# The first group of a seven-product matmul: half of its contraction by plain products in the order of arrival, and B loaded one block of rows at a time

## The chip, the cores and the metric

The kernel runs on one core of a Trainium2 chip. The time is the device time of the launch in microseconds (us), as a median of several executions. Ratios between kernels are the mean time of one kernel's fast runs over the mean of the other's in the same rounds, with a 95% interval, so they are not quite the ratio of the medians quoted beside them. Engines are named as in the profile: PE is TensorE, PEld its weight loads, DVE is VectorE, ACT is ScalarE, POOL is GpSimd. POOL issues the loads here.

## The reference

```python
m, k, n = 4096, 4096, 4096          # a and b: standard normal, float32
x = np.matmul(a, b)
return 0.5 * x * (1 + np.tanh(np.sqrt(2 / np.pi) * (x + 0.044715 * x**3)))
```

## The kernel before

Both matrices are cut into two by two quadrants, and each quadrant product is built from seven half-size products of sums instead of eight plain ones. The output is done in 16 groups of four 512 x 512 tiles (one in each quadrant). A group has 7 products; each runs over a contraction of 2048 in four quarters of 512, and a quarter is 16 matmuls of 128 x 128 by 128 x 512. DVE makes the fp16 sums of the operands (`aS`, `bS`) two steps ahead, and after each product DVE and ACT fold the result into the outputs (`settle`).

```python
PRODUCTS = [
    ("Y", "11", ("12", "22", 1)),          # needs B12 and B22 for its first sum
    ("X", ("11", "12", -1), "22"),
    ("X", ("12", "22", -1), ("21", "22", 1)),
    ("X", ("11", "22", -1), ("11", "22", -1)),
    ("X", "22", ("21", "11", 1)),
    ("Y", ("22", "21", -1), "11"),
    ("Y", ("21", "11", -1), ("11", "12", 1)),
]
```

A tile of A or B is 1024 contraction rows by 512, 1.05 MB in fp16, cast from float32 by the DMA. A tile of A is turned by a DVE transposition after it has landed. A tile of B comes in eight pieces of 128 KB: 32 partitions with 4 rows each.

```python
b_v = b.rearrange("(c g jj q e) n -> c g e q jj n", g=4, q=Q, e=2, jj=NJ // 2)   # Q = 32
...
for g in range(4):
    for e in range(2):
        nc.gpsimd.dma_start(
            out=t[g * Q : (g + 1) * Q, e::2, :],
            in_=b_v[kh * CH + c, g, e, :, :, n0 : n0 + NC],
        )
```

So partition 32 g + q holds the rows 256 g + 64 jj + 2 q + e of its chunk. That odd order is what the transposition of A gives, and B has to follow it.

Of the kernel before, what the change touches and what calls it, by code (L numbers as in the profile page):

```python
# [7 lines left out]
F32 = mybir.dt.float32  # L8
F16 = mybir.dt.float16
BF16 = mybir.dt.bfloat16  # L10
# [3 lines left out]
ALU = mybir.AluOpType  # L14
AX = mybir.AxisListType

P = 128
Q = 32
NC = 512
KC = 1024  # L20
NJ = KC // P
RUN = KC // 4
RT = 4
TM = RT * P
AHEAD = 2
# [12 lines left out]
]  # L38
NP = len(PRODUCTS)
QPH = 4  # L40


SQUARE_MAX = 2.0**26
# [45 lines left out]
def half_path(  # L89
# [9 lines left out]
    nc = tc.nc  # L99
    M, K = a.shape  # L100
    _, N = b.shape
# [3 lines left out]
    CH = KH // KC  # L105

    pool = ctx.enter_context(tc.tile_pool(name="sb", bufs=1))
    psum_pool = ctx.enter_context(tc.tile_pool(name="psum", bufs=1, space=bass.MemoryType.PSUM))
# [7 lines left out]
    checks = {which: iter(range(stats[which].shape[1] // NX)) for which in stats}  # L116

    a_v = a.rearrange("(x mm) (c g r) -> c g mm x r", mm=Q, g=4, r=RUN)
    b_v = b.rearrange("(c g jj q e) n -> c g e q jj n", g=4, q=Q, e=2, jj=NJ // 2)

    a_tiles, b_tiles = {}, {}
    a_slot = {"11": 0, "12": 1, "22": 2, "21": 3}
    b_slot = {"12": 0, "22": 1, "21": 2, "11": 3}
# [22 lines left out]
    def load_b(nb, quad, c):  # L146
        kh, jh = int(quad[0]) - 1, int(quad[1]) - 1
        n0 = jh * NH + nb * NC
        t = pool.tile([P, NJ, NC], F16, name="bR", tag=f"bR{b_slot[quad]}{c}")
        for g in range(4):  # L150
            for e in range(2):
                nc.gpsimd.dma_start(  # L152
                    out=t[g * Q : (g + 1) * Q, e::2, :],
                    in_=b_v[kh * CH + c, g, e, :, :, n0 : n0 + NC],
                )
        b_tiles[nb, quad, c] = t

    def part(tiles, blk, quad, q):

        t = tiles[blk, quad, q // 2].rearrange("p x y -> p (x y)")  # L160
        w = 4 * NC
        return t[:, (q % 2) * w : (q % 2 + 1) * w]

    energy, squares = {}, []
    W = 2 * NC
# [82 lines left out]
    def make_sums(mb, nb, s, q):  # L248
        _, oa, ob = PRODUCTS[s]
        got = []  # L250
        for tiles, blk, o, tag in ((a_tiles, mb, oa, "aS"), (b_tiles, nb, ob, "bS")):
            if isinstance(o, str):
                got.append(part(tiles, blk, o, q))
                continue
            t = pool.tile([P, 4 * NC], F16, name=tag, tag=tag, bufs=AHEAD + 1)
            nc.vector.tensor_tensor(  # L256
                out=t[:, :], in0=part(tiles, blk, o[0], q), in1=part(tiles, blk, o[1], q),
                op=ALU.add if o[2] > 0 else ALU.subtract,
            )
            got.append(t)  # L260
        sums[mb, nb, s, q] = got

    groups = []
# [5 lines left out]
    banks = {}  # L269
    post = {}  # L270

    def multiply(gi, s, q):
        mb, nb = groups[gi]
        chain = PRODUCTS[s][0]
        first = q == 0 and (s == 0 or s == 1)
        sa, sb = sums.pop((mb, nb, s, q))
        sa = sa.rearrange("p (jj m e) -> p jj m e", jj=2, e=2)
        sb = sb.rearrange("p (kt n) -> p kt n", n=NC)
        for i in range(RT):
            if first:  # L280
                par = (gi + (chain == "Y")) % 2
                banks[chain, i] = psum_pool.tile([P, NC], F32, name=f"acc{chain}", tag=f"bank{par}{i}")
            for j in range(4):
                nc.tensor.matmul(  # L284
                    banks[chain, i][:, :],
                    sa[:, j // 2, i * P : (i + 1) * P, j % 2],
                    sb[:, j, :],
                    start=first and j == 0,
                    stop=q == QPH - 1 and j == 3,
                    skip_group_check=True,  # L290
                )
            if q == QPH - 1:
                settle(gi, s, i)

    def keep(tag, src, bufs):
        t = pool.tile([P, NC], F32, name=tag, tag=tag, bufs=bufs)
        nc.scalar.copy(out=t[:, :], in_=src[:, :])  # L297
        return t
# [3 lines left out]
    def flush():  # L302

        for args in waiting:
            emit(*args)
        waiting.clear()
# [8 lines left out]
    def new_y():  # L315
        return pool.tile([P, NC], F32, name="y", tag="y", bufs=4)

    def tt(o, x, y, op):
        nc.vector.tensor_tensor(out=o[:, :], in0=x[:, :], in1=y[:, :], op=op)  # L319

    def settle(gi, s, i):

        X, Y = banks.get(("X", i)), banks.get(("Y", i))
        if s == 1:
            m5 = keep("m5", X, 2)
            flush()
            y = new_y()
            tt(y, Y, m5, ALU.subtract)
            waiting.append((gi, i, 0, 1, y, y))
        elif s == 2:  # L330
            post["x7", i] = keep("x7", X, RT)
        elif s == 3:
            x1 = post["x1", i] = keep("x1", X, RT)
            x7 = post["x7", i]
            tt(x7, x1, x7, ALU.subtract)
            tt(x1, Y, x1, ALU.subtract)
        elif s == 4:
            y = new_y()
            emit(gi, i, 0, 0, y, X)
            x1 = post["x1", i]  # L340
            tt(x1, X, x1, ALU.add)
        elif s == 5:
            y = new_y()
            tt(y, post.pop(("x1", i)), Y, ALU.subtract)
            flush()
            waiting.append((gi, i, 1, 0, y, y))
        elif s == 6:
            y = new_y()
            tt(y, Y, post.pop(("x7", i)), ALU.add)
            flush()  # L350
            waiting.append((gi, i, 1, 1, y, y))


    before = {}

    def at(gi, s, q, fn, *args):
        before.setdefault((gi * NP + s) * QPH + q, []).append((fn, args))


    T0 = -3  # L360
    for step, quads in (
        (-3, ("A11 0", "B12 0", "B22 0", "T11 0", "A11 1", "B12 1", "B22 1")),
        (0, ("T11 1", "A12 0", "A12 1")),
        (2, ("T12 0", "A22 0", "B21 0")),
        (4, ("T12 1", "A22 1", "B21 1", "B11 0")),
        (6, ("T22 0", "B11 1", "A21 0")),
        (8, ("T22 1", "A21 1")),
        (18, ("T21 0",)),
        (20, ("T21 1",)),
    ):  # L370
        for what in quads:
            fn = {"A": load_a, "B": load_b, "T": turn_a}[what[0]]
            at(0, 0, step, fn, 0, what[1:3], int(what[4]))


    nxt_b = {"12": "22", "22": "21", "21": "12", "11": "11"}
# [7 lines left out]
    for gi in range(len(groups) - 1):  # L384
        (mb, nb), (mb1, nb1) = groups[gi], groups[gi + 1]
        na, nbb = mb1 != mb, nb1 != nb
        if na:
            at(gi, 3, 0, move_slots, a_slot, nxt_a)
        if nbb:
            at(gi, 3, 0, move_slots, b_slot, nxt_b)  # L390
        for c in range(CH):
            if nbb:
                at(gi, 3, 2 * c + 1, load_b, nb1, "12", c)
                at(gi, 4, 2 * c + 1, load_b, nb1, "22", c)
                at(gi, 6, 2 * c + 1, load_b, nb1, "21", c)
            if na:
                at(gi, 4, c, load_a, mb1, "11", c)
                at(gi, 5, 2 * c, turn_a, mb1, "11", c)
                at(gi, 5, 2 * c + 1, load_a, mb1, "12", c)
                at(gi, 6, 2 * c, turn_a, mb1, "12", c)  # L400
                at(gi, 6, 2 * c + 1, load_a, mb1, "22", c)
                at(gi + 1, 0, 2 * c + 1, turn_a, mb1, "22", c)
                at(gi + 1, 1, c, load_a, mb1, "21", c)
                at(gi + 1, 3 + c, 0, turn_a, mb1, "21", c)
            if nbb:
                at(gi, 6, 2 * c + 1, load_b, nb1, "11", c)


    for mb in range(NMB):
        for which, gi in (("b", mb * NNB + 1), ("a", mb * NNB + 2)):  # L410
# [4 lines left out]
            ]  # L415
            n_two = len(pieces) - NP * QPH + 2
            for x, piece in enumerate(pieces):
                n = max(x // 2, x - n_two)
                at(gi, n // QPH, n % QPH, square, which, blk, *piece)
                at(gi, (n + 1) // QPH, (n + 1) % QPH, add_squares)  # L420
            at(gi, 6, 2, weigh, which)
# [16 lines left out]
    at(len(groups) - 1, 4, 0, read)  # L438

    with tc.manual_schedule():  # L440
        steps = [(gi, s, q) for gi in range(len(groups)) for s in range(NP) for q in range(QPH)]
        for n in range(T0, len(steps)):
            for fn, args in before.get(n, ()):
                fn(*args)
            if 0 <= n + AHEAD < len(steps):
                gi, s, q = steps[n + AHEAD]
                make_sums(*groups[gi], s, q)
            flush()
            if n >= 0:
                multiply(*steps[n])  # L450
        flush()
    return said["value"]

# [35 lines left out]
```

## Time and profile before

| | before |
|---|---|
| time, median of 4 | 1605.7 us |
| span of the profiled run | 1599.4 us |
| PE idle | 44.7 us, of it 34.2 before 75 us |
| first group over at | 138.0 us |
| packets of 4 bytes on the load queue | 15,360 |

The lines on PE, its waits and the first 40 us are in the prediction. Three more lines of the page are about the loads: the load queue (packets, MB, share of 16 engines' time), POOL's issue of B pieces (busy us, mean ns of one), and the time from issue to landing of such a piece.

```profile
q0 software_dynamic: 187392, 142.67, 61.1%
...
L152 POOL DMA_DIRECT2D bR<-in_b_dram x832 | 448.6, 544 | 720.2 <-DVE bS L256 357.8
...
bR<-in_b_dram POOLq DMA_DIRECT2D x832, 128.0 KB, 5.3
```

### The profile page before, as it was taken

To read this page: it belongs to the slowest core of one execution; us is meant where nothing else is said; L and a number is where in the kernel's file an instruction comes from. 1 tells how busy PE (TensorE), PEld (TensorE's weight loads), DVE (VectorE), ACT (ScalarE), POOL (GpSimd) and SP (SyncE) were. 2 spreads that over 40 slices of the span, in tenths; PEclk is the share of its full clock that TensorE was granted. 3 is DMA by queue.
4 is the path that set the end of the run, shared out by engine and by line. 5 is a ranking of instruction groups with operands and counts; after the bars stand their busy time and mean duration, and the time that the engine had idled before them with its cause. 6 is when DMAs were issued, how large, how long until landed. Compare 5 with 4: busy or idle time off the path is not lost. (4 is left out here: it accounts for less than half of the span.)

```text
span 1599.4 us, 19504 instructions
## 1 busy us (share of the span) xinstructions
PE 1554.7 (97%) x7168; PEld 702.9 (44%) x7168; DVE 1243.0 (78%) x1368; ACT 517.6 (32%) x706; POOL 530.8 (33%) x964
## 2 busy tenths in 40 slices
PE   2899999999999999999999999999999999999998
PEld 1344444444444444444444444444444444444443
DVE  2777888867977788886778788887687778888774
ACT  0114446412111644532112354542111144464111
POOL 6554341440323244332123414345021443414300
PEclk9999999999999999999999999999999999999999
DMA  9998674790967688488296847778477885747802
GB/s 179 198 201 158 105 147 99 129 207 29 196 100 144 138 132 158 86 154 156 56 181 106 174 82 137 151 117 182 81 127 137 132 158 101 149 94 132 157 27 81
DMA packets 224791, 211.12 MB, mean 132 GB/s; under 512 B 19888, under 2 KB 191920, under 8 KB 224688
## 3 DMA queue, kind: packets, MB, share of 16 engines
q0 software_dynamic: 187392, 142.67, 61.1%
q1 hardware_dynamic: 37296, 67.13, 11.6%
q8 instruction: 58, 0.95, 0.2%
q14 instruction: 45, 0.37, 0.1%
HBM read 285.22 MB, written 67.11 MB: 220 GB/s over the span
## 5 line engine op out<-in xcount | busy, mean ns | idle before, releaser
L284 PEld LDWEIGHTS <-aS 128*128 128x128 f16 x5120 | 501.4, 98 | 614.5 <-issue 9.1
L152 POOL DMA_DIRECT2D bR<-in_b_dram x832 | 448.6, 544 | 720.2 <-DVE bS L256 357.8
L256 DVE TENSOR_TENSOR aS<-aT 128x2048 f16<-128x2048 f16 x320 | 388.1, 1219 | 157.8 <-PE accX L284 121.9
L284 PE MATMUL accX<-bS,aS 128*128 128x512 f16 x2048 | 446.9, 380 | 8.6 <-DVE bS L256 7.4
L256 DVE TENSOR_TENSOR bS<-bR 128x2048 f16<-128x2048 f16 x320 | 387.7, 1218 | 80.2 <-PE accX L284 43.5
L284 PEld LDWEIGHTS <-aT 128*128 128x128 f16 x2048 | 201.5, 98 | 274.5 <-issue 23.1
L284 PE MATMUL accY<-bS,aT 128*128 128x512 f16 x1024 | 228.5, 385 | 29.1 <-DVE bS L256 29.1
L310 ACT ACTIVATE y<-y 128x512 f32<-128x512 f32 x192 | 118.6, 630 | 343.6 <-DVE y L319 343.3
L284 PE MATMUL accX<-bS,aT 128*128 128x512 f16 x1024 | 223.9, 379 | 0.0
L284 PE MATMUL accX<-bR,aS 128*128 128x512 f16 x1024 | 223.6, 379 | 0.0
L284 PE MATMUL accY<-bR,aS 128*128 128x512 f16 x1024 | 223.6, 379 | 0.0
L284 PE MATMUL accY<-bS,aS 128*128 128x512 f16 x1024 | 223.6, 379 | 0.0
L319 DVE TENSOR_TENSOR energy<-energy,square 128x1024 bf16<-128x1024 bf16 x240 | 164.6, 686 | 10.1 <-ACT square L177 6.4
L132 POOL DMA_DIRECT2D stage<-in_a_dram x128 | 82.0, 646 | 251.9 <-DVE aT L143 235.7
L297 ACT COPY x<-accX 128x512 f32<-128x512 f32 x128 | 75.1, 587 | 238.3 <-PE accX L284 238.3
L177 ACT ACTIVATE square<-aT 128x1024 bf16<-128x1024 f16 x120 | 123.9, 1051 | 64.6 <-DVE energy L319 64.3
L177 ACT ACTIVATE square<-bR 128x1024 bf16<-128x1024 f16 x120 | 123.5, 1051 | 60.5 <-DVE energy L319 60.5
L297 ACT COPY m<-accX 128x512 f32<-128x512 f32 x64 | 37.1, 580 | 248.7 <-PE accX L284 248.7
L143 DVE STREAM_TRANSPOSE aT<-stage 128x2048 uint32<-128x2048 uint32 x32 | 73.8, 2306 | 27.0 <-DMA stage<-in_a_dram 26.9
L319 DVE TENSOR_TENSOR x<-accX,x 128x512 f32<-128x512 f32 x64 | 44.3, 692 | 43.0 <-ACT y L310 43.0
L310 ACT ACTIVATE y<-accX 128x512 f32<-128x512 f32 x64 | 38.2, 597 | 119.6 <-PE accX L284 119.6
L319 DVE TENSOR_TENSOR y<-accY,m 128x512 f32<-128x512 f32 x64 | 42.7, 687 | 14.2 <-ACT m L297 14.2
(24 smaller groups left out, 224.0 us busy)
## 6 DMA issues: line engine op xcount, KB each, us to landing
bR<-in_b_dram POOLq DMA_DIRECT2D x832, 128.0 KB, 5.3
out_dram<-y SPq DMA_DIRECT2D x256, 256.0 KB, 5.4
stage<-in_a_dram POOLq DMA_DIRECT2D x128, 256.0 KB, 7.0
row<-seen_d SPq DMA_DIRECT2D x2, 1.5 KB, 2.1
seen_d<-seen SPq DMA_DIRECT2D x1, 3.0 KB, 7.3
```

The costliest lines, as they stand in the source:

```text
L132: nc.gpsimd.dma_start(out=s[g * Q : (g + 1) * Q, :, :], in_=a_v[kh * CH + c, g, :, x0 : x0 + TM // Q, :],)
L143: nc.vector.transpose(dst, src)
L152: nc.gpsimd.dma_start(out=t[g * Q : (g + 1) * Q, e::2, :], in_=b_v[kh * CH + c, g, e, :, :, n0 : n0 + NC],)
L177: nc.scalar.activation(t[:, :], src, ACT.Square)
L256: nc.vector.tensor_tensor(out=t[:, :], in0=part(tiles, blk, o[0], q), in1=part(tiles, blk, o[1], q), op=ALU.add if o[2] > 0 else ALU.subtract,
L284: nc.tensor.matmul(banks[chain, i][:, :], sa[:, j // 2, i * P : (i + 1) * P, j % 2], sb[:, j, :], start=first and j == 0, stop=q == QPH - ...
L297: nc.scalar.copy(out=t[:, :], in_=src[:, :])
L310: nc.scalar.activation(y[:, :], src[:, :], ACT.Gelu_apprx_tanh)
L319: nc.vector.tensor_tensor(out=o[:, :], in0=x[:, :], in1=y[:, :], op=op)
```

## The change

The intent: a sum-product can begin only when three tiles are there, a plain one when two are. For the first half of the first group's contraction, where PE waits for arrival, eight plain products replace the seven, in the order in which tiles come. The banks X and Y go on accumulating into the seven products of the second half; what the scheme would count wrongly is kept aside (`c12`, `c21`) and added at the end. Some zero products run first, to have the array at full clock when data comes. And B is loaded in pieces of one block of 128 contraction rows over all 128 partitions, so that the first quarter product needs half a tile.

```diff
+PLAIN = [
+    ("12", "11", "12"), ("11", "11", "11"), ("12", "12", "22"), ("11", "12", "21"),
+    ("21", "21", "11"), ("21", "22", "21"), ("22", "21", "12"), ("22", "22", "22"),
+]
+N_WARM = 28
...
-    b_v = b.rearrange("(c g jj q e) n -> c g e q jj n", g=4, q=Q, e=2, jj=NJ // 2)
+    b_v = b.rearrange("(c g jj q e) n -> c jj e g q n", g=4, q=Q, e=2, jj=NJ // 2)
...
-        for g in range(4):
-            for e in range(2):
-                nc.gpsimd.dma_start(
-                    out=t[g * Q : (g + 1) * Q, e::2, :],
-                    in_=b_v[kh * CH + c, g, e, :, :, n0 : n0 + NC],
-                )
+        for j in range(NJ):
+            nc.gpsimd.dma_start(
+                out=t[:, j, :], in_=b_v[kh * CH + c, j // 2, j % 2, :, :, n0 : n0 + NC]
+            )
...
+    def warm():                      # 28 matmuls of zeros into a bank not yet in use
...
+    def plain(n):                    # 16 matmuls; after a quadrant's last quarter:
+            if quad == "12":
+                post["c12", i] = keep("x7", acc, RT)                       # ACT copy
+            elif quad == "11":
+                tt(post["c12", i], post["c12", i], acc, ALU.add)           # DVE
+            elif quad == "21":
+                nc.scalar.copy(out=t[:, :], in_=acc[:, :])                 # ACT copy
+            else:
+                tt(post["c12", i], post["c12", i], acc, ALU.subtract)      # DVE
...
+            if gi == 0:
+                tt(y, y, post.pop(("c12", i)), ALU.add)      # second product of group 0
...
+            if gi == 0:
+                tt(x1, x1, post.pop(("c21", i)), ALU.add)    # fourth product of group 0
...
+    for n, whats in (
+        (0, "A11_0 B12_0 T11_0 B11_0 A12_0"),
+        (2, "B22_0"),
+        (4, "T12_0 B21_0 A21_0 A22_0"),
+        (8, "T21_0 B12_1 B22_1 A11_1"),
+        (10, "T22_0 A12_1"),
+        (14, "T11_1 A22_1 B21_1 B11_1"),
+        (16, "T12_1 A21_1"),
+        (18, "T22_1"),
+        (24, "T21_1"),
+    ):
```

(A and B are loads, T is the transposition of an A tile; the digit after the line is the half of the contraction, the number in front is the step.) The new pieces are used in all 16 groups; everything else concerns the first, apart from two early loads for the second.

More of the change, by code (lines that the diff above doesn't have):

```diff
@@ L40 @@
 QPH = 4
+PLAIN = [
+    ("12", "11", "12"), ("11", "11", "11"), ("12", "12", "22"), ("11", "12", "21"),
+    ("21", "21", "11"), ("21", "22", "21"), ("22", "21", "12"), ("22", "22", "22"),
+]
+N_PLAIN = 2 * len(PLAIN)
+N_WARM = 28
 SQUARE_MAX = 2.0**26
@@ L270, in half_path, with bank, products @@
     post = {}
+    def bank(gi, chain, i):
+        par = (gi + (chain == "Y")) % 2
+        t = psum_pool.tile([P, NC], F32, name=f"acc{chain}", tag=f"bank{par}{i}")
+        banks[chain, i] = t
+        return t
+    def products(acc, sa, sb, i, start, stop):
+        sa = sa.rearrange("p (jj m e) -> p jj m e", jj=2, e=2)
+        sb = sb.rearrange("p (kt n) -> p kt n", n=NC)
+        for j in range(4):
+            nc.tensor.matmul(
+                acc[:, :], sa[:, j // 2, i * P : (i + 1) * P, j % 2], sb[:, j, :],
+                start=start and j == 0, stop=stop and j == 3, skip_group_check=True,
+            )
+    def warm():
+        z = pool.tile([P, NC], F16, name="zeros", tag="bS", bufs=AHEAD + 1)
+        nc.vector.memset(z[:, :], 0.0)
+        for i in range(RT):
+            bank(0, "X", i)
+            bank(0, "Y", i)
+        for _ in range(N_WARM):
+            nc.tensor.matmul(
+                banks["X", RT - 1][:, :], z[:, :P], z[:, :], start=True, stop=True, skip_group_check=True
+            )
+    def plain(n):
+        (quad, oa, ob), q = PLAIN[n // 2], n % 2
+        chain = "X" if quad == "11" else "Y"
+        seen = [x for x in range(len(PLAIN)) if PLAIN[x][0] == quad]
+        start = n == 2 * seen[0]
+        stop = n == 2 * seen[-1] + 1
+        for i in range(RT):
+            acc = banks[chain, i]
+            products(acc, part(a_tiles, 0, oa, q), part(b_tiles, 0, ob, q), i, start, stop)
+            if not stop:
+                continue
+            if quad == "12":
[3 more added lines that the diff above has]
+            elif quad == "21":
+                tag = ("energy1", "energy2", "square", "square")[i]
+                t = pool.tile([P, W], BF16, name="c21", tag=tag, bufs=1 + (i > 1)).bitcast(F32)
+                nc.scalar.copy(out=t[:, :], in_=acc[:, :])
+                post["c21", i] = t
+            else:
+                tt(post["c12", i], post["c12", i], acc, ALU.subtract)
     def multiply(gi, s, q):
@@ L276, in multiply @@
         sa, sb = sums.pop((mb, nb, s, q))
-        sa = sa.rearrange("p (jj m e) -> p jj m e", jj=2, e=2)
-        sb = sb.rearrange("p (kt n) -> p kt n", n=NC)
         for i in range(RT):
-            if first:
-                par = (gi + (chain == "Y")) % 2
-                banks[chain, i] = psum_pool.tile([P, NC], F32, name=f"acc{chain}", tag=f"bank{par}{i}")
-            for j in range(4):
-                nc.tensor.matmul(
-                    banks[chain, i][:, :],
-                    sa[:, j // 2, i * P : (i + 1) * P, j % 2],
-                    sb[:, j, :],
-                    start=first and j == 0,
-                    stop=q == QPH - 1 and j == 3,
-                    skip_group_check=True,
-                )
+            acc = bank(gi, chain, i) if first else banks[chain, i]
+            products(acc, sa, sb, i, first, q == QPH - 1)
             if q == QPH - 1:
@@ L351, in settle @@
             waiting.append((gi, i, 1, 1, y, y))
+    steps = [(0, -1, n) for n in range(N_PLAIN)]
+    steps += [(0, s, q) for s in range(NP) for q in range(QPH // 2, QPH)]
+    steps += [(gi, s, q) for gi in range(1, len(groups)) for s in range(NP) for q in range(QPH)]
+    position = {step: n for n, step in enumerate(steps)}
     before = {}
     def at(gi, s, q, fn, *args):
-        before.setdefault((gi * NP + s) * QPH + q, []).append((fn, args))
-    T0 = -3
-    for step, quads in (
-        (-3, ("A11 0", "B12 0", "B22 0", "T11 0", "A11 1", "B12 1", "B22 1")),
-        (0, ("T11 1", "A12 0", "A12 1")),
-        (2, ("T12 0", "A22 0", "B21 0")),
-        (4, ("T12 1", "A22 1", "B21 1", "B11 0")),
-        (6, ("T22 0", "B11 1", "A21 0")),
-        (8, ("T22 1", "A21 1")),
-        (18, ("T21 0",)),
-        (20, ("T21 1",)),
+        if gi == 0 and s >= 0:
+            q = max(q, QPH // 2)
+        before.setdefault(position[gi, s, q], []).append((fn, args))
+    for n, whats in (
[8 more added lines that the diff above has]
+        (24, "T21_1"),
     ):
-        for what in quads:
+        for what in whats.split():
             fn = {"A": load_a, "B": load_b, "T": turn_a}[what[0]]
-            at(0, 0, step, fn, 0, what[1:3], int(what[4]))
+            before.setdefault(n, []).append((fn, (0, what[1:3], int(what[4]))))
     nxt_b = {"12": "22", "22": "21", "21": "12", "11": "11"}
@@ L389, in half_path @@
         if nbb:
-            at(gi, 3, 0, move_slots, b_slot, nxt_b)
+            at(gi, 3 - (gi == 0), 0, move_slots, b_slot, nxt_b)
         for c in range(CH):
             if nbb:
-                at(gi, 3, 2 * c + 1, load_b, nb1, "12", c)
-                at(gi, 4, 2 * c + 1, load_b, nb1, "22", c)
+                early = gi == 0 and c == 0
+                at(gi, 3 - early, 2 * c + 1, load_b, nb1, "12", c)
+                at(gi, 4 - early, 2 * c + 1, load_b, nb1, "22", c)
                 at(gi, 6, 2 * c + 1, load_b, nb1, "21", c)
@@ L440, in half_path @@
     with tc.manual_schedule():
-        steps = [(gi, s, q) for gi in range(len(groups)) for s in range(NP) for q in range(QPH)]
-        for n in range(T0, len(steps)):
+        warm()
+        for n, step in enumerate(steps):
             for fn, args in before.get(n, ()):
                 fn(*args)
-            if 0 <= n + AHEAD < len(steps):
+            if n + AHEAD < len(steps):
                 gi, s, q = steps[n + AHEAD]
-                make_sums(*groups[gi], s, q)
+                if s >= 0:
+                    make_sums(*groups[gi], s, q)
             flush()
-            if n >= 0:
-                multiply(*steps[n])
+            if step[1] < 0:
+                plain(n)
+            else:
+                multiply(*step)
         flush()
```

## The prediction

> **What bounds the kernel now.** I read the page first, for the engine that is nearly full.
>
> ```profile
> span 1599.4 us, 19504 instructions
> PE 1554.7 (97%) x7168; PEld 702.9 (44%) x7168; DVE 1243.0 (78%) x1368; ACT 517.6 (32%) x706; POOL 530.8 (33%) x964
> ```
>
> TensorE (PE) is idle for 1599.4 - 1554.7 = 44.7 us in all. Nothing that removes waits alone can gain more than that, and 2% of 1606.1 us would be 32 us. So I next read the view of who waited for whom, for PE, to see where the 44.7 us lie.
>
> ```profile
> engine line waited for: us in total, times, longest us
> PE accY L284 <- DVE bS L256: 29.1, 2, 22.6
> PE accX L284 <- DVE bS L256: 7.4, 2, 4.0
> PE accX L284 <- ACT m L297: 1.1, 1, 1.1
> ```
>
> Five waits make 37.6 us; the remaining 7.0 us are the tail after the last matmul. Asked in windows, one wait of 3.4 us is near 1525 us (the verdict on the magnitudes); the other four, 34.2 us, all lie before 75 us, in the first of 16 groups. The timeline of that stretch shows what each hangs on.
>
> ```profile
> start us, us, engine line op out<-in xcount [idle before <-releaser]
> ...
> 10.77 2.31 DVE L143 STREAM_TRANSPOSE aT<-stage 128x2048 uint32<-128x2048 uint32 x1 [10.77 <-DMA stage<-in_a_dram]
> ...
> 21.32 2.36 DVE L256 TENSOR_TENSOR bS<-bR 128x2048 f16<-128x2048 f16 x2 [8.24 <-DMA stage<-in_a_dram]
> 22.60 9.08 PE L284 MATMUL accY<-bS,aT 128*128 128x512 f16 x32 [22.60 <-DVE bS L256]
> ...
> 26.52 2.31 DVE L143 STREAM_TRANSPOSE aT<-stage 128x2048 uint32<-128x2048 uint32 x1 [2.84 <-DMA stage<-in_a_dram]
> ...
> 36.93 2.36 DVE L256 TENSOR_TENSOR bS<-bR 128x2048 f16<-128x2048 f16 x2 [8.10 <-DMA stage<-in_a_dram]
> 38.21 9.80 PE L284 MATMUL accY<-bS,aT 128*128 128x512 f16 x32 [6.53 <-DVE bS L256]
> ```
>
> The first product needs a sum of two B tiles besides a turned A tile, so three tiles of 1.05 MB must land before PE starts at 22.6 us. Tiles land 5.2 us apart: third 21.3, fourth 26.5, sixth 36.9, seventh 42.3 us. The start is bound by arrival; DMA is full there (about 200 GB/s in nearly every slice). A last view gives the busy time on each side of the first group's end.
>
> ```profile
> 0.00:138.00 138.00, 103.74 (x449) 45.52 (x449) 82.65 (x73) 17.79 (x28) 83.28 (x152) 0.96 1.18 189
> 138.00:1592.40 1454.40, 1450.97 (x6721) 657.42 (x6719) 1159.68 (x1295) 498.56 (x677) 447.50 (x813) 1.00 0.69 127
> ```
>
> Columns after the length are busy PE, weight loads, DVE, ACT, POOL. Once past 138.0 us PE simply streams: 1454.4 us for 6720 matmuls, 216 ns each. In the first group 448 matmuls at that rate are 96.8 us, the waits are 34.2, and the remaining 7 us are matmuls at half speed: after the start, the 6.53 us gap and the 4.0 us gap, about 10, 13 and 9 matmuls are 427 ns apart.
>
> **What the Trainium skill says.** "TensorE: Matmul & The Clock Gate", Part 1, says that the array starts at half clock, is released after some 3.4 us of sustained work and falls back after an idle window of that length. The trace agrees: 427 against 216 ns, cold runs of roughly 4 to 5.5 us, none after the gap of 1.1 us. The same page, under the architectural detail, says VectorE takes its queue in strict order; that matters below, and the trace contradicts nothing of it. "DMA: Bandwidth & Descriptors", on why a DMA increments its semaphore by 16 ("How many engines"), has a transfer spread over the largest number up to 16 that divides the slow dimension: 32 partitions (old B load) and 128 (new) both give 16 engines, so I expect no change of rate from the shape. "Perfetto Trace Analysis", DMA Optimizations, says smaller chunks may allow some to start sooner; here the piece stays 128 KB, but each new piece is one block of 128 contraction rows, so half a tile suffices for a quarter product.
>
> **The change, part by part.**
> *Removed:* for the first half of the first group's contraction, 7 sum-products of 32 matmuls each (224) and their 20 DVE sums of 1.2 us. *Added:* 8 plain products (256 matmuls), so +32 x 0.216 = 6.9 us on PE; 28 matmuls on zeros, before any data is there and so beside the loads; 8 DVE additions of 0.69 us into the stored halves and 8 more at the end, 8 ACT copies of 0.58. *Moved:* load order, and B pieces throughout. Groups 2 to 16 keep their matmuls and were without waits but the one at 1525 us, so I leave them at 1454.4 us and work out only when the first group ends.
>
> Arrival of tile n, from the landings above: 10.8 + 5.23(n-1). Transposition adds 2.3.
> - A11 10.8, turned 13.1; half of B12 about 13.4. PE starts real work at 13.5 instead of 22.6. The zero products take 10 x 0.427 + 18 x 0.216 = 8.2 us from about 1.5 us, over by 10.
> - Each plain product is 32 x 0.216 = 6.9 us. P1 ends 20.4; P2 needs B11 (half 18.6, whole 21.2), ends 27.3. P3 needs A12 (26.5, turned 28.8) and half of B22 (29.1): wait 1.9, ends 36.1. P4 has B21 (half 34.3): ends 43.0.
> - P5 needs A21, landed 42.1. But in DVE's order the four additions of P4's result stand before its transposition; the last is done about 43.9, so it is turned at 46.2: wait 3.3. P5 to P8 then run through: 73.9.
> - Remaining half, 7 x 6.9 = 48.4 us. Its tiles are numbers 9 to 16, 52.6 to 89.2; each is there before use. DVE is now the tight one: 20 sums (24 us), 8+24 post operations on 128x512 (22 us), four transpositions (9 us) stand against 48 us of PE. At the fourth product 12 operations instead of 8 follow each other: from 100.3 at 0.665 (the 8 took 94.79 to 100.10) to 108.2; then the last transposition and one sum to 111.8, while PE finished the fifth at 108.9: wait 2.9. The sixth product ends 118.7; DVE, behind two more sums, four post additions, four sums and the first reading of the Y bank, releases that bank at 120.9: wait 2.2. Some 0.5 us goes at the third product, where ACT copies alternate with GELU.
> - End of the group: 13.5 + 480 x 0.216 (103.7) + waits 1.9 + 3.3 + 0.5 + 2.9 + 2.2 (10.8) = 128.0, against 138.0.
> - Half clock: the idle 9.7 to 13.5 and the 3.3 us before P5 are near the length that made PE cold (4.0 did, 1.1 did not). I choose a half and a third chance of some 2 us each: +1.7.
>
> Sum: 138.0 - 129.7 = 8.3 us less, so 1606.1 - 8.3, about **1598 us**.
>
> **The rivals.**
> 1. *All of the 34 us goes.* If every wait vanished, and the cold 7 us with it, the net would be 34.2 + 7 - 6.9 - 13.5 for the first arrival, some 21 us: 1585. Against it: the two DVE queues above and arrival at P3. I expect the DVE additions to eat what the earlier start wins.
> 2. *The new B pieces issue slower.* POOL takes 0.54 us for a 32-partition piece; nothing in this trace shows one over 128 partitions. At 1 us a tile of eight would take 8 us to issue, over the 5.2 it takes to land, and P2 to P4 would each wait 3 us: 1605. In later groups POOL, 33% busy, would still be hidden.
> 3. *DVE becomes the bound further than I count*, because head-of-queue waits add up, or the group after it starts with late sums: waits of 20 instead of 10.8 us, 1606.
> 4. *The matmul count rules:* only +6.9 us, if the arrival stays the bound to the end of the group (16 tiles at 89 us, seven half-products of work after the last but few). Against: 16 tiles land by 89 us, where PE still has 39 us of work.
>
> **Range and chances.** Pieces of either sign: arrivals +-1 us, cold 0 to 4, DVE waits +-4, POOL up to +7. I take 1598 with 1590 to 1605. Faster by over 2% would need 32 us, more than the rival without any waits gives; slower would need as much lost. Both are remote: 0.015 and 0.01.
>
> **What would show it.** In the changed trace: first data matmul at 13 to 14 us; a wait of about 2 us before the third product and 3 before the fifth, the latter released by a transposition on DVE; P8's end near 74; a wait near 109 and one near 119 us behind DVE; the first group over near 128 to 130; no waits from there to 1500. PE would count 60 more matmuls. B pieces at 0.54 us on POOL would settle the second rival. I am wrong if the start slips (pieces land in another order than issued), if the rate of the loads moves by the new shape, or if later groups gain or lose waits.

## The result, and the profile after

The changed kernel takes **1615.05 us** (1614.18 to 1616.03, 4 runs) against 1605.71 us (1604.22 to 1607.43, 4 runs): ratio 1.0058, interval 1.0041 to 1.0075. That is 0.6% slower where 0.5% faster was predicted, and outside the predicted range of 1590 to 1605.

The page of the changed kernel, its head and then the three lines shown of the kernel before:

```profile
span 1612.5 us, 19459 instructions
PE 1571.8 (97%) x7228; PEld 709.2 (44%) x7228; DVE 1229.2 (76%) x1365; ACT 522.5 (32%) x714; POOL 636.9 (39%) x964
...
q0 software_dynamic: 506880, 143.95, 74.3%
...
L159 POOL DMA_DIRECT2D bR<-in_b_dram x832 | 554.5, 672 | 657.0 <-DMA bR<-in_b_dram 237.5
...
bR<-in_b_dram POOLq DMA_DIRECT2D x832, 128.0 KB, 7.4
```

The matmul count is as expected, 60 more. The bytes are the same within 1%, but the packets more than doubled (544,279 in the whole run), and all the 319,488 new ones are under 512 bytes (packets of 4 bytes on the load queue before: 15,360). POOL takes 672 instead of 544 ns to issue a piece, and a piece takes 7.4 instead of 5.3 us to land.

PE's timeline in the first 60 us, without the zero products at its start and the fifth product at its end (start, length, what, and in brackets the idle time before it and what ended it):

```profile
15.64 8.47 PE L289 MATMUL accY<-bR,aT 128*128 128x512 f16 x32 [6.39 <-DVE aT L151]
23.94 4.26 PE L289 MATMUL accX<-bR,aT 128*128 128x512 f16 x19
28.48 2.97 PE L289 MATMUL accX<-bR,aT 128*128 128x512 f16 x13 [0.27 <-DMA bR<-in_b_dram]
38.46 8.99 PE L289 MATMUL accY<-bR,aT 128*128 128x512 f16 x32 [7.01 <-DVE aT L151]
47.29 7.07 PE L289 MATMUL accX<-bR,aT 128*128 128x512 f16 x32
```

The third product, which was to start at 29, starts at 38.5 after 7 us of idling for the turned A12. The transposition is not at fault: DVE had been idle for 20.5 us and began when the loads let it, at 36.09 us instead of the 26.5 that the landings of before gave. Three transpositions of that run, of A11, of A21 and of A11's second half, show when their tiles were there:

```profile
13.27 2.31 DVE L151 STREAM_TRANSPOSE aT<-stage 128x2048 uint32<-128x2048 uint32 x1 [12.01 <-DMA stage<-in_a_dram]
...
55.95 2.31 DVE L151 STREAM_TRANSPOSE aT<-stage 128x2048 uint32<-128x2048 uint32 x1 [0.79 <-DMA stage<-in_a_dram]
...
85.76 2.31 DVE L151 STREAM_TRANSPOSE aT<-stage 128x2048 uint32<-128x2048 uint32 x1 [21.02 <-DMA stage<-in_a_dram]
```

A11's second half is the eleventh tile, predicted for 63.1. That is 7.25 us a tile from the first to the eleventh, not 5.23.

What the load queue moved from 14 to 60 us says the same: first the kernel before, then the changed one.

```profile
DMA packets 13559, 8.70 MB, mean 189 GB/s; under 512 B 787, under 2 KB 13557, under 8 KB 13557
```

```profile
DMA packets 20865, 6.95 MB, mean 151 GB/s; under 512 B 11097, under 2 KB 20864, under 8 KB 20864
```

PE's waits in the changed kernel, from 15 us on to the first group's last product, and then those of the stretch 140 to 200 us that fall in the second group:

```profile
PE accY L289 <- DVE aT L151: 17.4, 3, 7.0
PE accY L289 <- DVE x L364: 3.2, 1, 3.2
PE accY L289 <- DVE aS L262: 3.0, 1, 3.0
PE accX L289 <- ACT m L342: 1.5, 2, 1.1
```

```profile
PE accY L289 <- DVE bS L262: 3.1, 2, 1.9
```

(The 17.4 include the 6.4 us between the zeros and the first data product.) The first group is over at 147.27 us instead of 138.0; the second loses 3.1 us to two late `bS` sums; from 200 to 1400 us there is no wait. Nowhere does the slower load show again. The 13.1 us of longer span are 9.3 in the first group and 3.8 in the rest (those 3.1, and products at half clock after them).

### The profile page after: what moved, and what is told of

It is laid out like the page before. It is cut to its first block, busy times and chain, and to the rows that moved or that the text cites. A ratio compares the mean times of both kernels' runs of the same rounds, so it can differ in the third digit from the quotient of the medians.

```text
span 1612.5 us, 19459 instructions
## 1 busy us (share of the span) xinstructions
PE 1571.8 (97%) x7228; PEld 709.2 (44%) x7228; DVE 1229.2 (76%) x1365; ACT 522.5 (32%) x714; POOL 636.9 (39%) x964
## 2 busy tenths in 40 slices
DMA packets 544279, 212.40 MB, mean 132 GB/s; under 512 B 339376, under 2 KB 511408, under 8 KB 544176
## 5 line engine op out<-in xcount | busy, mean ns | idle before, releaser
L159 POOL DMA_DIRECT2D bR<-in_b_dram x832 | 554.5, 672 | 657.0 <-DMA bR<-in_b_dram 237.5
L289 PEld LDWEIGHTS <-aS 128*128 128x128 f16 x4960 | 485.5, 98 | 595.3 <-DVE aS L262 6.3
L262 DVE TENSOR_TENSOR aS<-aT 128x2048 f16<-128x2048 f16 x310 | 375.9, 1219 | 149.7 <-PE accX L289 116.0
L289 PE MATMUL accX<-bS,aS 128*128 128x512 f16 x1984 | 431.3, 379 | 4.9 <-DVE bS L262 3.5
L262 DVE TENSOR_TENSOR bS<-bR 128x2048 f16<-128x2048 f16 x310 | 375.5, 1218 | 60.4 <-PE accX L289 41.0
L289 PEld LDWEIGHTS <-aT 128*128 128x128 f16 x2240 | 220.5, 99 | 294.5 <-DVE aT L151 19.6
L289 PE MATMUL accY<-bS,aT 128*128 128x512 f16 x992 | 218.3, 381 | 6.2 <-DVE x L364 3.2
L289 PE MATMUL accX<-bS,aT 128*128 128x512 f16 x992 | 217.0, 379 | 0.0
L289 PE MATMUL accY<-bS,aS 128*128 128x512 f16 x992 | 216.7, 379 | 0.2 <-DVE y L364 0.2
L289 PE MATMUL accY<-bR,aT 128*128 128x512 f16 x192 | 47.0, 410 | 17.4 <-DVE aT L151 17.4
```

The lines of the kernel that those rows point to most:

```text
L159: nc.gpsimd.dma_start(out=t[:, j, :], in_=b_v[kh * CH + c, j // 2, j % 2, :, :, n0 : n0 + NC])
L262: nc.vector.tensor_tensor(out=t[:, :], in0=part(tiles, blk, o[0], q), in1=part(tiles, blk, o[1], q), op=ALU.add if o[2] > 0 else ALU.subtract,
L289: nc.tensor.matmul(acc[:, :], sa[:, j // 2, i * P : (i + 1) * P, j % 2], sb[:, j, :], start=start and j == 0, stop=stop and j == 3, skip_g ...
```

## The experiments

Two theories stood at the start. **Shape:** the new B pieces, with all their small packets, slow the arrival, and the plain schedule itself is as good as predicted. **Schedule:** the plain products, their extra 6.9 us of matmuls and the additional DVE work are what cost. Ten kernels were run.

### Only the pieces, and only the products

`e1_plain_old_pieces`: the changed kernel with the view and the loop of pieces of the kernel before (the `-` lines of the second and third hunk of the diff put back).

> The changed kernel with B loaded in the pieces of the kernel before (32 partitions x 4 rows). Theory (the new shape of the B pieces, 128 partitions x 1 row, with its extra 4-byte packets, slows arrival from 5.2 to about 7.3 us a tile): packets back to about 225,000, tiles 5.2 us apart, first group over near 131 us, time about 1600 us (1597 to 1604). Rival (the plain schedule itself, its DVE queue and its 32 extra products, is what costs): time stays at 1611 to 1616 us.

Measured: 1598.23 us (1596.43 to 1599.38), before on the same chip 1604.25; ratio 0.9968 (0.9943 to 0.9993). The first group is over at 131.4 us.

`e2_seven_new_pieces`: the kernel before with those two hunks alone applied.

> The kernel before with only the B pieces of the changed one. Theory: arrival slows here too, packets rise to about 544,000, the two long waits of the first group grow, time about 1618 us (1612 to 1625), while groups 2 to 16 stay without waits. Rival: the shape is hidden, within 3 us of 1606.

Measured: 1624.44 us (1621.11 to 1625.1); ratio 1.0122 (1.0095 to 1.0149). The packets are 544,279, exactly those of the changed kernel; PE's wait before the second half of the first product grew from 6.5 to 13.4 us. No wait lies between 150 and 1400 us.

So the shape of the pieces costs some 20 us with the old products and 14 to 17 us with the new ones (14 by the ratios 0.9968 and 1.0058, 17 by medians of different rounds), nearly all of it in the first group or just after it. The plain products by themselves are a gain of 5 to 6 us. The schedule theory has fallen.

### The prediction's own kernel

With the old pieces a quarter product has to wait for a whole tile, which the prediction did not assume. `e3_plain_by_parity` gets half-tile arrival with old pieces: the pieces of even rows first, then odd, and the plain quarters go over even and odd rows instead of over the first and second half.

```diff
-        for g in range(4):
-            for e in range(2):
+        for e in range(2):
+            for g in range(4):
                 nc.gpsimd.dma_start(out=t[g * Q : (g + 1) * Q, e::2, :], ...)
...
-            products(acc, part(a_tiles, 0, oa, q), part(b_tiles, 0, ob, q), i, start, stop)
+            sa = a_tiles[0, oa, 0].rearrange("p jj (m e) -> p jj m e", e=2)
+            sb = b_tiles[0, ob, 0]
+            for jj in range(4):
+                nc.tensor.matmul(acc[:, :], sa[:, jj, i * P : (i + 1) * P, q], sb[:, 2 * jj + q, :], ...)
```

(The diff is against `e1_plain_old_pieces`.)

> Old pieces, sent even rows first, and the plain quarter products taken over even and odd contraction rows, so that half a tile still suffices for a quarter. Theory: the arithmetic of the prediction holds once tiles land 5.2 us apart: first data product at 13 to 14 us, first group over near 128 to 130 us, time about 1598 us (1594 to 1602), 2 to 3 us under the plain kernel with old pieces. Rival: as that one or slower, 1611 to 1616.

Measured: 1594.69 us (1593.13 to 1595.36); ratio 0.9940 (0.9915 to 0.9965). PE's timeline, the first 60 us and the end of the first group (the last line is the second group's first product):

```profile
12.42 9.99 PE L319 MATMUL accY<-bR,aT 128*128 128x512 f16 x32 [3.22 <-DMA bR<-in_b_dram]
...
29.15 7.07 PE L319 MATMUL accY<-bR,aT 128*128 128x512 f16 x32
36.06 7.07 PE L319 MATMUL accX<-bR,aT 128*128 128x512 f16 x32
46.20 14.10 PE L319 MATMUL accY<-bR,aT 128*128 128x512 f16 x58 [3.08 <-DVE aT L151]
```

```profile
113.29 8.77 PE L291 MATMUL accY<-bR,aS 128*128 128x512 f16 x32 [3.00 <-DVE aS L264]
121.95 7.07 PE L291 MATMUL accY<-bS,aS 128*128 128x512 f16 x32
128.85 6.42 PE L291 MATMUL accY<-bS,aT 128*128 128x512 f16 x29
```

With tiles arriving at the old rate, the prediction's table holds nearly line by line: third product at 29.15 (29.2 predicted), fourth over at 43.1 (43.0), a wait of 3.08 before the fifth (3.3), one of 3.00 before the sixth sum product (2.9), group over at 128.85 (129.7 with the half-clock allowance). Two terms were off and cancel, which is luck: the first data product starts at 12.42 us, before the 13 to 14 expected, and it ran cold and took 9.8 us instead of 6.9, so the wait of 1.9 us before the third product does not show. The 2.2 us before the last product do not show either, because the product ahead of it ran slowly.

### What it is about the shape

Two things are new in a piece: it covers 128 partitions with one row each, and the source is read as 4 blocks of 32 rows, because of the order in which partitions hold rows. The sizes recorded for each packet let one count. On the load queue of the two kernels:

```
               4 bytes   512 bytes   1024 bytes
before          15,360      65,536      106,496
changed        334,848      65,536      106,496
```

Data packets are the same. An A piece costs 16 packets of 4 bytes in both (128 pieces), so a B piece costs 16 before and 400 after: 384 more, three for each of its 128 rows. My first reading was that rows are made up to four per partition. `e5_pairs` loads the same 128 KB as 64 partitions x 2 rows:

```diff
-    b_v = b.rearrange("(c g jj q e) n -> c jj e g q n", g=4, q=Q, e=2, jj=NJ // 2)
+    b_v = b.rearrange("(c g jj q e) n -> c jj g q e n", g=4, q=Q, e=2, jj=NJ // 2)
...
-        for j in range(NJ):
-            nc.gpsimd.dma_start(out=t[:, j, :], in_=b_v[kh * CH + c, j // 2, j % 2, :, :, n0 : n0 + NC])
+        for j in range(NJ // 2):
+            for k in range(2):
+                nc.gpsimd.dma_start(
+                    out=t[64 * k : 64 * k + 64, 2 * j : 2 * j + 2, :],
+                    in_=b_v[kh * CH + c, j, 2 * k : 2 * k + 2, :, :, n0 : n0 + NC],   # 2 blocks of 64 rows
+                )
```

> The changed kernel with B in pieces of 64 partitions x 2 rows, the same 128 KB and 128 rows of 1 KB. Reading of the traces so far: 4 rows per partition gave 16 packets of 4 bytes a piece, 1 row gave 400, that is 3 more for each of the 128 partitions, as if rows were made up to 4 per partition. If so: 2 more for each of 64 partitions, 144 a piece, and 121,856 packets of 4 bytes in all on the load queue (832 x 144 + 128 x 16), and arrival a third of the way, tiles about 5.9 us apart, time about 1600 to 1605 us. Rival, any piece over more than 32 partitions gets 3 more per partition: 208 a piece. Rival, it is the spread over partitions that is slow and not the packets: time as the changed kernel, 1612 to 1616.

Measured: **1758.73 us** (1756.83 to 1764.0); ratio 1.0966 (1.0946 to 1.0986). Every expectation missed. The 4-byte packets are 760,832 in all, 912 a piece, seven for each row. The load queue, POOL's issue and the landing of that run:

```profile
q0 software_dynamic: 932864, 145.65, 86.3%
...
L160 POOL DMA_DIRECT2D bR<-in_b_dram x832 | 1073.6, 1296 | 345.6 <-DMA bR<-in_b_dram 214.8
...
bR<-in_b_dram POOLq DMA_DIRECT2D x832, 128.0 KB, 10.9
```

The slower load is no longer hidden in the middle groups here: from 200 to 1400 us PE waits 50.5 us in all for `bS` sums.

Zero, three and seven extra packets a row fit 16/k - 1 with k = 16, 4 and 2. Now 32, 4 and 2 are the first dimension of the source as the three kernels give it to the DMA (32 x 4 x 512, 4 x 32 x 512, and 2 blocks of 64 rows x 512). The Trainium skill, "DMA: Bandwidth & Descriptors", on why a DMA increments its semaphore by 16 ("How many engines"), says that the number of engines is the largest up to 16 that divides the slowest dimension of each of the two access patterns. I had applied that to the tile's side alone. If it is the cause, a tile loaded with exactly the new pieces, but from a source with another first dimension, must lose the extra packets. `e9_one_stride` and `e10_eight_blocks` do that by reading other rows, so their results are wrong (relative error 1.16; the index of a piece changes with the view); sizes, counts, buffers and schedule are those of the changed kernel.

```diff
 # e9_one_stride: source 128 x 512
-    b_v = b.rearrange("(c g jj q e) n -> c jj e g q n", g=4, q=Q, e=2, jj=NJ // 2)
+    b_v = b.rearrange("(c v w) n -> c w v n", v=P, w=NJ)
 # e10_eight_blocks: source 8 x 16 x 512
+    b_v = b.rearrange("(c u h v w) n -> c h w u v n", u=8, h=2, v=16, w=4)
```

> The changed kernel, tile and pieces as they are (128 partitions x 1 row), but the 128 rows of a piece read from DRAM with one stride, 128 x 512, and not as 4 blocks of 32 rows. The rows go to the wrong places, so the result is wrong on purpose; sizes, counts and buffers are the same. Theory: the number of engines is the largest up to 16 that divides the slowest dimension of both sides (here 128 and 128, in the changed kernel 4 and 128, in the pairs 2 and 64), and each row costs 16/k - 1 extra packets of 4 bytes: 3 for k = 4 (seen: 384 = 128 x 3), 7 for k = 2 (seen: 896 = 128 x 7). Then none here: 15,360 packets of 4 bytes on the load queue, tiles about 5.2 us apart, time about 1595 us (1592 to 1599). Rival, one row per partition or 128 partitions is what is slow: as the changed kernel, 334,848 packets, 1612 to 1616 us.

> The same with the rows read as 8 blocks of 16 (wrong result on purpose, again). Theory: k = 8, one extra packet a row, 144 of 4 bytes a piece, 121,856 on the load queue; time between one stride and four blocks, about 1596 to 1606 us. Rival, any source in two steps is slow whatever its first size: as the changed kernel, 1612 to 1616.

Measured: 1594.38 us (1592.1 to 1595.93), ratio 0.9930 (0.9911 to 0.9949), and 1596.60 us (1595.52 to 1597.55), ratio 0.9945 (0.9928 to 0.9962). The 4-byte packets are 15,360 and 121,856, both to the packet as expected. Their lines, one stride first:

```profile
q0 software_dynamic: 187392, 142.67, 60.9%
...
L159 POOL DMA_DIRECT2D bR<-in_b_dram x832 | 443.8, 538 | 719.0 <-DVE bS L262 336.5
...
bR<-in_b_dram POOLq DMA_DIRECT2D x832, 128.0 KB, 5.2
```

```profile
q0 software_dynamic: 293888, 143.09, 66.9%
...
L159 POOL DMA_DIRECT2D bR<-in_b_dram x832 | 484.7, 609 | 692.0 <-DVE bS L262 220.9
...
bR<-in_b_dram POOLq DMA_DIRECT2D x832, 128.0 KB, 5.8
```

All under the same plain schedule (the GB/s are of the stretch 14 to 60 us; the last row has another piece on the tile's side too):

| source of a piece | k that fits | 4-byte packets a row | POOL per piece | landing | GB/s | time |
|---|---|---|---|---|---|---|
| 128 x 512 | 16 | 0 | 538 ns | 5.2 us | 190 | 1594.4 us |
| 8 x 16 x 512 | 8 | 1 | 609 ns | 5.8 us | 173 | 1596.6 us |
| 4 x 32 x 512 (the change) | 4 | 3 | 672 ns | 7.4 us | 151 | 1615.1 us |
| 2 x 64 x 512 | 2 | 7 | 1296 ns | 10.9 us | 104 | 1758.7 us |

So neither the 128 partitions nor the one row per partition is slow; the split of the source is. Three things stay open. The trace does not record which engine moved a packet, so that k engines carried the data is the page's statement, and what is shown is that its rule gives the packet counts exactly in all five shapes tried, two of them forecast. The tile's side had 32, 64 or 128 partitions, all multiples of 16, so only the source's side of the rule was varied; and the last two kernels read other rows of DRAM, so that their times might also hang on the addresses; their counts came out as forecast. And the extra packets, the longer issue and the supposed smaller number of engines always come together, so which of them lengthens the landing was not told apart. The traces narrow it: from 14 to 60 us POOL was busy 30.2 us with k = 16 and 28.0 with k = 4, and there its waits ended with landings, so at k = 4 the longer issue is hardly the limit. And the 4-byte packets of that stretch made up 12% of the recorded packet time with k = 4 against 2% with k = 16, while the rate fell by a fifth, so their own time does not account for all of it.

### The zero products

`e4_parity_no_zeros` is the kernel by parity with `N_WARM = 0`, `e6_zeros_to_data` the same with `N_WARM = 42`.

> The same by parity without the 28 zero products. If the zeros keep the array warm for the first data product: about 2 us slower than with them, about ten matmuls 427 ns apart at the start. If the array has gone cold again in the gap between zeros and data: no difference beyond 0.5 us.

> By parity, with 42 zero products instead of 28, so that they end near 12.3 us, when the first half tile is there, and not at 9.2. Theory, the zeros did nothing because the array fell back to half clock in the 3.2 us between: first product in 7.1 instead of 10.0 us, 2 to 3 us less than with 28 zeros or none, about 1592 us. Rival, the clock at the start does not reach the end of the group because arrival holds the second and third product anyway: within 0.7 us.

Measured: without zeros 1593.83 us (1593.77 to 1595.5), ratio 0.9941, the same as with 28 (0.9940). With 42: 1595.27 us (1592.38 to 1598.28), ratio 0.9936 (0.9921 to 0.9951): again no difference that can be told. The reasons differ. The 28 zeros end at 9.2 us, and after the 3.2 us until data comes the array is cold again: 9.99 us for the first product in the timeline above. The 42 do last until data, and the first product takes 7.07 us; but then the second is over earlier, PE waits 2.26 us for A12 before the third, and that one runs at half clock. One window of that run, the start of the third product (columns: length, then busy time of PE, PEld, DVE, ACT and POOL, the granted PE clock, and DMA share and GB/s):

```profile
29.50:33.00 3.50, 3.48 (x11) 1.37 (x12) 0.00 (x0) 0.00 (x0) 2.73 (x6) 0.66 1.24 202
```

The third product starts at 29.52 us with 42 zeros, at 29.15 with 28 and at 28.80 with none. Where PE waited for it, a landing (0.29 us of waiting with no zeros) or the turned A12 (2.26 us with 42) set that start, and the time saved on the first product was waited away.

### The two waits behind DVE's queue

`e7_turns_first` moves two transpositions ahead of DVE work that stood before them; `e8_turns_first_zeros` has 42 zeros as well.

```diff
-        (8, "T21_0 B12_1 B22_1 A11_1"),
+        (7, "T21_0"),
+        (8, "B12_1 B22_1 A11_1"),
...
-        (24, "T21_1"),
+        (23, "T21_1"),
```

> By parity, with two transpositions moved ahead of DVE additions in its queue: A21's first half before the four additions after the fourth plain product, A21's second half before the twelve operations after the fourth sum product. Theory, head of the queue: waits of 3.1 and 3.0 us fall to about 1 each, some 4 us less than by parity without it, about 1590.5 us. Rival, the twelve operations only push the wait to the next product, behind which DVE is just as late: 2 us or less.

> Both of the last two together. If they are independent, about 6 us less than by parity alone, near 1588 to 1589 us, 1.0% under the kernel before; if the start is swallowed by arrival, as turns first alone.

Measured: 1591.01 us (1589.92 to 1592.12), ratio 0.9913 (0.9900 to 0.9926), and 1590.18 us (1587.87 to 1590.85), ratio 0.9906 (0.9891 to 0.9921). PE's timeline of `e7_turns_first` at the end of the group:

```profile
108.81 7.08 PE L291 MATMUL accY<-bR,aS 128*128 128x512 f16 x32 [1.58 <-DVE aS L264]
117.47 7.07 PE L291 MATMUL accY<-bS,aS 128*128 128x512 f16 x32 [1.58 <-DVE y L372]
124.38 5.99 PE L291 MATMUL accY<-bS,aT 128*128 128x512 f16 x27
```

The waits of 3.08 and 3.00 became 1.70 and 1.58, and the group is over at 124.4 instead of 128.85. So 2.8 us of the 4.5 are waits; another 1.4 is the four products after the first of these gaps, which now run at full clock. The wait of 1.58 before the last product looks like part of the gain coming back, as the rival said, but the run without zeros has it too, behind an unchanged 3.00:

```profile
113.23 7.08 PE L291 MATMUL accY<-bR,aS 128*128 128x512 f16 x32 [3.00 <-DMA bR<-in_b_dram]
121.89 7.07 PE L291 MATMUL accY<-bS,aS 128*128 128x512 f16 x32 [1.58 <-DVE y L372]
```

In `e3_plain_by_parity` the product before it ran at half clock, 8.7 us instead of 7.1, and hid it. So the move did not lengthen that wait, and the rival did not come out. By ratios in the same rounds it is 0.9913 against 0.9936 with 42 zeros and no move. The two together are not told from the move alone. Either beats both given kernels: about 15 us, 0.9%, under the kernel before and 24 us under the changed one.

## Why the prediction was wrong

**The step that failed** is in its paragraph on the skill: "32 partitions (old B load) and 128 (new) both give 16 engines, so I expect no change of rate from the shape". I read one access pattern of the two. The source of a new piece begins with a dimension of 4, visible in the changed view of `b` (`g` before `q`), and with it the landing of a piece went from 5.3 to 7.4 us. From there the line "Arrival of tile n ... 10.8 + 5.23(n-1)" had the wrong slope: it was 13.3 + 7.25(n-1), from A tiles 1 and 11.

What that did to the sum, term by term, up to the end of the first group (129.7 predicted, 147.3 measured, 17.6 more):

- First data product: 15.6 us instead of 13.5, 2.1 more.
- Waits after it: 19.1 us instead of 10.8, 8.3 more. The third product waited 7.0 instead of 1.9, and a wait of 3.2 us came at the start of the second half, where the eleventh tile was late. The third sum product waited 1.5 instead of 0.5. The waits behind DVE's queue were nearly right: 3.95 before the fifth product (3.3 predicted), of which the last 0.79 is A21's late landing, and 3.0 before the sixth sum product (2.9). Before the last, 2.2 were predicted and 0.2 came, the product ahead of it having run slowly.
- Half clock: the rest, 147.3 - 15.6 - 19.1 - 103.7 = 8.9 us against 1.7 allowed, 7.2 more. It follows from the waits: the products after five of the gaps took 1.3 to 1.9 us longer than 6.9 each.

Then 3.1 us of waits in the second group and about 0.7 at half clock, where the prediction had none, for the same reason; 17.6 + 3.8 is the whole 21.4 us between -8.3 and +13.1 of span.

**Right:** that the whole gain has to come before 75 us and cannot reach 2%; that the middle groups have slack for the slower load (no waits from 200 to 1400 us with the change, though the pairs, slower still, used it up); the two longest waits that DVE's order of queue would make, 3.3 and 2.9 us (3.08 and 3.00 in the kernel by parity), while the 2.2 before the last product were 1.58 or hidden; and, as that kernel shows, the sum for a load of unchanged rate: 9.6 us under the kernel before by the ratio (5.6 to 13.6), where 8.3 was predicted. That it came out so close line by line is in part the luck told of there.

**The rivals.** The second, slower pieces, is what happened, but by another way and with another size: POOL needs 0.67 us a piece, not 1, while the landings grew by 2 us each, and the prediction stopped it at 1605. The third and fourth did not happen. I gave the second rival a room of up to 7 us in the range, although nothing in the trace of before showed a piece of that shape. A term that no row of the trace covers should have widened the range on that side by more, all the more as it stood under the first term of the sum.

## What to carry to other kernels

A view of DRAM that delivers the data in a better order can be a slower transfer with the same bytes, rows and row length: here a first dimension of 2, 4 or 8 on the source's side cost extra packets, one of 32 or 128 did not. So look at the first dimension of both sides of every DMA; that it should be a multiple of 16 is the rule of the page cited above, of which only these cases are shown. When the number of packets on a queue jumps while its bytes stay, ask for the shape of the pieces before anything else. And where work is gated by arrival, filling the array's idle time can change nothing, as the zeros did here: first ask which landing the next product waits for.

## What the Trainium skill lacked or had wrong

- "DMA: Bandwidth & Descriptors", on how many engines a DMA uses: the rule is there, and the table of rules names one case on the source's side, a broadcast, but the examples beside the rule speak of a tile's partitions ("a 128- or 96-partition tile"). A 128-partition tile fed from a source of 4 x 32 rows got 400 packets of 4 bytes a piece, from one of 128 rows 16. A plain load with a split source is the example that is lacking.
- The same page says that few engines confine a transfer, but has no measurement of what that costs and nothing of the extra packets. Here pieces of 128 KB issued by POOL had 16/k - 1 extra packets of 4 bytes for each 1 KB row, and landed in 5.2, 5.8, 7.4 and 10.9 us for k = 16, 8, 4 and 2, with 538, 609, 672 and 1296 ns of POOL for each.
- "TensorE: Matmul & The Clock Gate", Part 1, puts the fall to half clock after an idle window of about 3.4 us. In the run with 42 zeros a gap of 2.26 us was enough: matmuls came 427 ns apart from 1.5 us after it, at a granted clock of 0.66 between 29.5 and 33 us. The length of the gap does not decide alone: one of 3.00 us before the sixth sum product was followed by half clock in `e3_plain_by_parity` and `e6_zeros_to_data` (that product took 8.77 us) and by full clock in `e1_plain_old_pieces` and `e4_parity_no_zeros` (7.08 us). Gaps of 1.58 us were harmless.
